# Up projection of a gated MLP by seven block products in place of eight, down projection in groups of two

## The chip, the cores and the metric

One core of one Trainium2 chip runs the whole program. The time is device microseconds of one execution of the program, from the first instruction to the last; the time before is the median of three runs. TensorE (PE in the profile; its weight loads are PEld) multiplies, VectorE (DVE) and ScalarE (ACT) work on tiles in SBUF and read PSUM, GpSimd (POOL) works on SBUF only, and SyncE (SP) issues most DMAs.

## The reference

A decoder layer on 2048 tokens of 1024 channels: a norm, an input projection, three token mixers, an output projection, then the gated MLP with a convolution of width 3 along the tokens, then a per-layer embedding and a last norm. The change touches the MLP:

```python
def conv_ffn(h, w_up, conv_w, w_down):
    gu = causal_dwconv(h @ w_up, conv_w)      # h: 2048 x 1024, w_up: 1024 x 5632
    g, u = jnp.split(gu, 2, axis=-1)
    return (jax.nn.silu(g) * u) @ w_down      # w_down: 2816 x 1024
...
x = x + conv_ffn(rmsnorm(x, norm_ffn_gain[i]), ffn_w_up[i], ffn_conv_w[i], ffn_w_down[i])
```

All data is float32.

## The kernel before

The sequence is worked in two halves of 1024 tokens, each in two chunks of 512 (`NC`). Channels lie on the 128 partitions, so x is eight tiles of 1024 tokens, and a projection's output comes channel tile by channel tile, tokens along the free axis. The loop `for hf in range(NH)` runs the mixers, the output projection, the MLP and the embedding of one half and then of the other.

Every operand of a large product is kept as two float32r parts, high and low: `split` (L151) copies the high part on ScalarE (L153) and subtracts it on VectorE for the low part (L154). `mm3` (L159) makes one float32 product of three matmuls, high by high, high by low, low by high (L160 to L162). One projection of a channel tile on one chunk is 8 x 3 matmuls of 512 columns into one PSUM bank.

Weights come in the order of their use (`wlist`). `w_issue` (L131) loads one raw tile through SP's queue into one of two raw buffers and splits it; `w_next` keeps two more in hand than the one taken. Split weights have their own pool of four double tiles (`wp`); activations share the 32 tiles of `bp`.

In the MLP, `up(j)` (L708) projects two channel tiles, j of g and j of u, into one double PSUM bank each (`mm`, two of them), on both chunks. `conv` (L299) reads PSUM: ScalarE applies the first tap (L303), VectorE the two others (L307), with two columns of the tokens before (L309) or for the tokens after (L311). Then SiLU on ScalarE (L737), the gate product (L738) and a split into `ahi` and `alo`. `down(js)` takes up to three such tiles (`JG = 3`): for each of eight output tiles and two chunks it accumulates 3 x 3 matmuls in one of four single banks (`sm`) and VectorE adds the bank to x (L753). The order of `up` and `down` is that of `ffn_order`; the last group is one tile, and its `down` also splits x for the next stage. The first `up` is spread so that the norm of the second chunk (`Norm.rstd`, `bcast`, `h_apply`, L317) has work of the first beside it.

The order written is a priority only. A planner sets each engine's order ahead of the run: an instruction whose inputs or whose buffer are not ready by its estimate is passed by a later one, so a weight split stands between two steps of a convolution and the MLP's first matmuls stand between the last of the output projection. Tiles of a pool are given to whoever comes when one is free.

Of the kernel before, what the change touches and what calls it, by code (L numbers as in the profile page):

```python
# [11 lines left out]
I32 = mybir.dt.int32  # L12
# [19 lines left out]
JG = 3  # L32

# columns of the per-channel vectors: one column per 128 channels
# [8 lines left out]
# columns of the shape-only constants  # L43
# [5 lines left out]
def trunk(ctx, tc, xT, pT, w_in, w_out, w_up, w_down, w_pp, w_pg, wr_bd, wi_bd, vecs, consts, masks, out):  # L49
# [3 lines left out]
    wp = ctx.enter_context(tc.tile_pool(name="wp", bufs=4))  # L53
    bp = ctx.enter_context(tc.tile_pool(name="bp", bufs=32))
# [38 lines left out]
    wlist = []  # L93

    def ffn_order():
        ev = []
        groups = [list(range(j0, min(j0 + JG, NJ))) for j0 in range(0, NJ, JG)]
        for gi, js in enumerate(groups):
            for i, j in enumerate(js):
                ev.append(("up", j, None))  # L100
                if gi > 0 and i == (0 if gi < len(groups) - 1 else len(js) - 1):
                    ev.append(("down", gi - 1, groups[gi - 1]))
        ev.append(("down", len(groups) - 1, groups[-1]))
        return ev

    def down_per(js):
        return {1: 8, 2: 4, 3: 2, 4: 2}[len(js)]
# [7 lines left out]

    IN_UNITS = [9, 6, 12, 15, 10, 7, 13, 16, 11, 8, 14, 0, 3, 1, 4, 2, 5, 20, 22, 18, 21, 23, 19, 17]
    for hf in range(NH):
        wlist += [kc(w_in[m]) for m in IN_UNITS]
        wlist += [kc(w_out[m]) for _ in range(NC) for m in range(KD)]
        for ev, i, js in ffn_order():  # L120
            if ev == "up":
                wlist += [kc(w_up[i]), kc(w_up[NJ + i])]
            else:
                per = down_per(js)
                for m0 in range(0, KD, per):
                    wlist.append(w_down[m0 : m0 + per, :, js[0] : js[-1] + 1, :].rearrange("m p j c -> p m (j c)"))
        wlist += [kc(w_pg[m]) for _ in ple_chunks(hf == NH - 1) for m in range(KD)]
    wq = []
    wpos = [0]

    def w_issue():  # L131
        if wpos[0] >= len(wlist):
            return
        src = wlist[wpos[0]]
        wpos[0] += 1
        w = wp.tile([P, 2, D], F32R, tag="w", name=nm("w"))
        raw = wp.tile([P, D], F32, tag="wr", name=nm("wr"), bufs=2)
        dst, n = raw, D
        if len(src.shape) == 3:
            n = src.shape[1] * src.shape[2]  # L140
            dst = dst[:, :n].rearrange("p (a b) -> p a b", b=src.shape[2])
        nc.sync.dma_start(dst, src)
        split(w[:, 0, :n], w[:, 1, :n], raw[:, :n])
        wq.append(w)

    def w_next(ahead=2):
        while len(wq) <= ahead and wpos[0] < len(wlist):
            w_issue()
        return wq.pop(0)

    def split(hi, lo, src, eng=None):  # L151
        """hi + lo <- src, in two float32r parts; src is float32."""
        i = ACT(hi, src, AF.Copy)  # L153
        last_split[:] = i, (eng or nc.vector).tensor_tensor(lo, src, hi.bitcast(F32), op=SUB)  # L154

    def wsl(w, k):
        return w[:, 0, k * P : (k + 1) * P], w[:, 1, k * P : (k + 1) * P]

    def mm3(ps, wk, rk, start, stop):  # L159
        MM(ps, wk[0], rk[0], start=start, stop=False)  # L160
        MM(ps, wk[0], rk[1], start=False, stop=False)  # L161
        MM(ps, wk[1], rk[0], start=False, stop=stop)  # L162
# [29 lines left out]
    class Norm:  # L192
        """1/rms over the channels of 512 tokens."""
# [36 lines left out]
    def head_norm(y, gain, scale=1.0):  # L230
        """y <- rmsnorm over each head's 64 channels of (scale * y), times gain; gain has scale in it."""
# [14 lines left out]
    def head_sum(parts, name):  # L246
        """1/64 of the sum over each head's 64 channels, on all of them."""
# [43 lines left out]
    rgw = cp.tile([P, 2, 2, 3, P], F32R, name="rgw")  # L291
    mk = cp.tile([P, NL - 1, C], I32, name="mk")
# [6 lines left out]
    def conv(dst, src, taps, bias, tail, first, last):  # L299
        """causal depthwise convolution along the free axis; taps[d]: the weight at delay d."""  # L300
# [12 lines left out]
    def h_apply(dst, xs, gain, pr, pool=()):  # L313
        """dst[k] <- xs[k] * gain * pr, in two parts; the k in pool have one step on GpSimd."""
# [56 lines left out]
    for hf in range(NH):  # L371
# [336 lines left out]
        def up(j, head=False):  # L708
# [10 lines left out]
            if head:  # L719
                for i in range(2):  # L720
                    ws[i], pss[i] = w_next(), ps2("pu2")
# [205 lines left out]
```

## Time and profile before

| | |
|---|---|
| median of three runs | 2584.52 us (2583.66 to 2589.34) |
| span of the profiled execution | 2585.0 us |
| first and last matmul of the MLP's up projection, both halves | 458 us, 2413 us |
| DMA over the span | 168.40 MB, mean 65 GB/s |
| instructions | 29876 |

The profile is of one execution. A row of a group gives the line, the engine, the operation, output and inputs, shapes and count; then the busy time, the mean of one instruction in ns, the idle time of the engine just before them, and what ended that. The ends of matmuls are modelled, and rows of matmuls overlap. The granted clock is given as a share of full speed. In a timeline, the first number is the start from the span's begin and the second the duration.

### The profile page before, as it was taken

To read this page: it belongs to the slowest core of one execution; us is meant where nothing else is said; L and a number is where in the kernel's file an instruction comes from. 1 tells how busy PE (TensorE), PEld (TensorE's weight loads), DVE (VectorE), ACT (ScalarE), POOL (GpSimd) and SP (SyncE) were. 2 spreads that over 40 slices of the span, in tenths; PEclk is the share of its full clock that TensorE was granted. 3 is DMA by queue.
4 is the path that set the end of the run, shared out by engine and by line. 5 is a ranking of instruction groups with operands and counts; after the bars stand their busy time and mean duration, and the time that the engine had idled before them with its cause. 6 is when DMAs were issued, how large, how long until landed. Compare 5 with 4: busy or idle time off the path is not lost.

```text
span 2585.0 us, 29876 instructions
## 1 busy us (share of the span) xinstructions
PE 2544.2 (98%) x12508; PEld 2106.3 (81%) x12508; DVE 1411.1 (55%) x1984; ACT 958.2 (37%) x1170; POOL 79.9 (3%) x94
## 2 busy tenths in 40 slices
PE   7999999999999999999999999999999999999998
PEld 5888788788888888888888887888888888888888
DVE  7666565653453443447666655665443453453666
ACT  5444873422122222224444458633222222121344
POOL 3000000200000000000110000000000000000000
PEclk9999999999999999999999999999999999999999
DMA  4111014321111111113420011331111111111224
GB/s 143 34 33 34 33 65 135 109 76 41 56 51 41 56 43 49 55 43 131 139 89 34 25 33 41 102 127 35 55 49 44 55 43 50 56 34 58 80 88 141
DMA packets 64663, 168.40 MB, mean 65 GB/s; under 512 B 6160, under 2 KB 27920, under 8 KB 64528
## 3 DMA queue, kind: packets, MB, share of 16 engines
q1 hardware_dynamic: 58960, 149.09, 17.7%
q0 software_dynamic: 4992, 16.78, 1.9%
q8 instruction: 98, 1.61, 0.3%
q10 hardware_dynamic: 576, 0.62, 0.1%
q14 instruction: 37, 0.30, 0.0%
HBM read 158.08 MB, written 8.39 MB: 64 GB/s over the span
## 4 chain that ended last, share of the span: by engine, by line
PE 90%; ACT 5%; DVE 3%; issue 1%; DMA 1%; POOL 0%; SPq 0%; DVEq 0%; POOLq 0%; ACTq 0%
PE pu L160 12%; PE pu L161 12%; PE pu L162 12%; PE pdn L160 6%; PE pdn L162 6%; PE pdn L161 6%; PE pz L160 5%; PE pz L161 5%; PE pz L162 5%; PE pgt L160 2%; PE pgt L161 2%; PE pgt L162 2%; PE po L160 2%; PE po L161 2%; PE po L162 2%; PE pl L535 2%
## 5 line engine op out<-in xcount | busy, mean ns | idle before, releaser
L160 PE MATMUL pu<-h,w 128*128 128x512 f32 x1408 | 548.5, 390 | 2.9 <-DVE ftail L311 2.6
L161 PE MATMUL pu<-h,w 128*128 128x512 f32 x1408 | 549.0, 390 | 0.6 <-POOL h L154 0.4
L162 PE MATMUL pu<-h,w 128*128 128x512 f32 x1408 | 548.2, 390 | 0.0
L307 DVE SCALAR_TENSOR_TENSOR gu<-pu,vt,gu 128x1023 f32<-128x1023 f32 (+1 forms) x176 | 225.1, 1279 | 517.3 <-ACT gu L303 517.3
L153 ACT ACTIVATE w<-wr 128x1024 fp32r<-128x1024 f32 (+1 forms) x266 | 267.9, 1009 | 381.9 <-PE pdn L162 299.0
L154 DVE TENSOR_TENSOR w<-wr,w 128x1024 fp32r<-128x1024 f32 (+1 forms) x266 | 309.8, 1165 | 48.4 <-ACT w L153 47.8
L160 PEld LDWEIGHTS pu<-h,w 128*128 128x128 f32 x1408 | 264.5, 188 | 58.3 <-ACT w L153 3.0
L161 PEld LDWEIGHTS pu<-h,w 128*128 128x128 f32 x1408 | 264.5, 188 | 57.4 <-POOL h L154 2.7
L160 PE MATMUL pz<-h,w 128*128 128x512 f32 x768 | 307.6, 401 | 2.5 <-ACT h L153 2.3
L162 PEld LDWEIGHTS pu<-h,w 128*128 128x128 f32 x1408 | 264.5, 188 | 54.7
L161 PE MATMUL pz<-h,w 128*128 128x512 f32 x768 | 303.4, 396 | 2.0 <-DVE h L154 1.7
L162 PE MATMUL pz<-h,w 128*128 128x512 f32 x768 | 301.4, 393 | 0.0
L160 PE MATMUL pdn<-ahi,w 128*128 128x512 f32 x704 | 274.3, 390 | 0.0
L162 PE MATMUL pdn<-ahi,w 128*128 128x512 f32 x704 | 274.3, 390 | 0.0
L161 PE MATMUL pdn<-alo,w 128*128 128x512 f32 x704 | 274.2, 390 | 0.0
L303 ACT ACTIVATE gu<-pu,vt 128x1024 f32<-128x1024 f32 x88 | 98.2, 1116 | 449.6 <-PE pu L162 449.6
L753 DVE TENSOR_TENSOR x<-x,pdn 128x512 f32<-128x512 f32 x256 | 173.0, 684 | 155.3 <-PE pdn L162 154.9
L160 PEld LDWEIGHTS pz<-h,w 128*128 128x128 f32 x768 | 145.4, 189 | 34.1 <-ACT h L153 3.6
L161 PEld LDWEIGHTS pz<-h,w 128*128 128x128 f32 x768 | 145.4, 189 | 34.0 <-DVE h L154 4.6
L162 PEld LDWEIGHTS pz<-h,w 128*128 128x128 f32 x768 | 145.3, 189 | 30.0
L162 PEld LDWEIGHTS pdn<-ahi,w 128*128 128x128 f32 x704 | 132.2, 188 | 27.5
L160 PEld LDWEIGHTS pdn<-ahi,w 128*128 128x128 f32 x704 | 132.2, 188 | 27.5
(218 smaller groups left out, 3088.8 us busy)
## 6 DMA issues: line engine op xcount, KB each, us to landing
wr<-in_w_up SPq DMA_DIRECT2D x88, 512.0 KB, 3.3
wr<-in_w_in SPq DMA_DIRECT2D x48, 512.0 KB, 3.3
wr<-in_w_down SPq DMA_DIRECT2D x56, 384.0 KB, 3.3
wr<-in_w_pg SPq DMA_DIRECT2D x40, 512.0 KB, 3.3
wr<-in_w_out SPq DMA_DIRECT2D x32, 512.0 KB, 3.4
xr<-in_xT POOLq DMA_DIRECT2D x32, 256.0 KB, 3.2
out_y<-o SPq DMA_DIRECT2D x24, 256.0 KB, 2.5
xl<-in_xT SPq DMA_DIRECT2D x8, 512.0 KB, 8.1
```

Of the source, the lines that this page charges most:

```text
L153: i = ACT(hi, src, AF.Copy)
L154: last_split[:] = i, (eng or nc.vector).tensor_tensor(lo, src, hi.bitcast(F32), op=SUB)
L160: MM(ps, wk[0], rk[0], start=start, stop=False)
L161: MM(ps, wk[0], rk[1], start=False, stop=False)
L162: MM(ps, wk[1], rk[0], start=False, stop=stop)
L303: ACT(dst, src, AF.Copy, scale=taps[0])
L307: STT(dst[:, d:TH], src[:, 0 : TH - d], taps[d], dst[:, d:TH], op0=MUL, op1=ADD)
L535: MM(pl[:, t * P : (t + 1) * P], K[:, tk : tk + P], qz[:, c * 4 + t].rearrange("p a b -> p (a b)"), start=True, stop=True)
L753: TT(x[m][:, cks(c)], x[m][:, cks(c)], ps, op=ADD)
```

## The change

For each channel tile pair but the first of each half, the eight block products of the up projection become seven. The blocks are: channel tiles g and u (weights wg, wu), halves of the 1024 input channels (a, b), and token chunks (0, 1). The inputs X1 and X2 are the halves of chunk 0, X3 the second half of chunk 1, and X4 to X7 sums and differences of the four, made once in `h2_first` and `h2_second`; the weights of products 3, 5, 6 and 7 are sums and differences of the four quarters of a raw pair, made for every tile by `job_s` on VectorE and then split. Products 1, 6, 7 and 4 accumulate into one bank A that is copied between them. The convolution reads the sums from SBUF. The first pair of each half uses `up_first`, eight products of which two have a difference of inputs.

Down groups are of two tiles, then two of one. Weights are named jobs in one list and taken with `w_get`, two jobs ahead. MLP weights take tiles of the pool `ff`, which is opened before the output projection with nine tiles; all other weights take tiles of `bp`, which has 40. Mask and gate weights of the mixers lie in the mixers' pool and are loaded in each half. The scratch for DMAs issued by GpSimd is smaller.

```diff
-    wp = ctx.enter_context(tc.tile_pool(name="wp", bufs=4))
-    bp = ctx.enter_context(tc.tile_pool(name="bp", bufs=32))
+    wp = ctx.enter_context(tc.tile_pool(name="wp", bufs=2))
+    bp = ctx.enter_context(tc.tile_pool(name="bp", bufs=40))
...
+    GROUPS = [[j, j + 1] for j in range(0, NJ - 2, 2)] + [[NJ - 2], [NJ - 1]]
...
+    def job_a(hf, j):
+        g = raws[hf, j, 0] = raw_w(kc(w_up[j]))
+        raws[hf, j, 1] = raw_w(kc(w_up[NJ + j]))
+        hi, lo = ftile("wh", F32R), ftile("wl", F32R)
+        split(hi, lo, g)
+        return hi, lo
...
+    def job_s(hf, j, which):
+        g, u = raws[hf, j, 0], raws[hf, j, 1]
+        hi, lo = ftile("wh", F32R), ftile("wl", F32R)
+        q = [slice(0, CH), slice(CH, D)]
+        if which == 0:
+            s = raws[hf, j, 2] = sp.tile([P, D], F32, tag="s", name=nm("s"), bufs=1)
+            TT(s[:, q[0]], u[:, q[0]], u[:, q[1]], op=ADD)
+            TT(s[:, q[1]], s[:, q[0]], g[:, q[0]], op=SUB)
+        else:
+            s = raws[hf, j, 2]
+            TT(s[:, q[0]], g[:, q[1]], s[:, q[1]], op=SUB)
+            TT(s[:, q[1]], g[:, q[0]], u[:, q[0]], op=SUB)
+        split(hi, lo, s)
+        return hi, lo
+
+    def job_a22(hf, j):
+        t = ftile("w22", F32R)
+        split(t[:, :CH], t[:, CH:], raws[hf, j, 1][:, CH:])
+        return t
...
+        for j in range(NJ):
...
+            wlist += [(("a", *a), lambda a=a: job_a(*a))]
+            wlist += [(("s", *a, i), lambda a=a, i=i: job_s(*a, i)) for i in range(2)]
...
+            if j % 2 == 0:
+                wlist.append(down[0])
+            wlist.append((("a22", *a), lambda a=a: job_a22(*a)))
+            if j % 2 == 0:
+                wlist.append(down[1])
...
+        def h2_second(pr):
...
+            for q in range(KQ):
+                hx(h1[q], q, 1, pr)
+                TT(h0[q], h1[q], h0[q], op=SUB)
+                X[5][q] = split_chunk(h0[q], "h")
+            yield
+            for q in range(KQ):
+                hx(h1[KQ + q], KQ + q, 1, pr)
+                X[3][q] = split_chunk(h1[KQ + q], "h")
+            yield
+            for q in range(KQ):
+                TT(h0[q], h1[KQ + q], h0[q], op=SUB)
+                nc.gpsimd.tensor_tensor(h1[q], h1[KQ + q], h1[q], op=SUB)
+                X[6][q] = split_chunk(h0[q], "h")
+            yield
+            for q in range(KQ):
+                nc.gpsimd.tensor_tensor(h0[KQ + q], h0[KQ + q], h0[q], op=SUB)
+                X[7][q] = split_chunk(h1[q], "h")
+            yield
+            for q in range(KQ):
+                X[4][q] = split_chunk(h0[KQ + q], "h")
...
+        def prod(ps, w, xs_, start, stop):
+            for q in range(KQ):
+                mm3(ps, (w[0][:, q * P : (q + 1) * P], w[1][:, q * P : (q + 1) * P]), hsl(xs_[q]),
+                    start and q == 0, stop and q == KQ - 1, skip_group_check=True)
...
+        def up(j, between):
+            A, BC = ps1(name="pa"), ps2("pbc")
+            B, Cc = BC[:, C0], BC[:, C1]
+            zg, zu = ftile("zg"), ftile("zu")
+
+            def p1():
+                prod(A, wa[0], X[1], True, False)
+                ACT(zg[:, C0], A, AF.Copy)
+
+            def p2():
+                prod(Cc, wa[1], X[2], True, True)
+                TT(zg[:, C0], zg[:, C0], Cc, op=ADD)
+
+            def p5():
+                prod(B, ws[0], X[5], True, False)
+                ACT(zu[:, C1], B, AF.Copy)
+
+            def p6():
+                prod(A, ws[1], X[6], False, False)
+                ACT(zg[:, C1], A, AF.Copy)
+
+            def p3():
+                prod(B, wt[0], X[3], False, True)
+                TT(zg[:, C1], zg[:, C1], B, op=ADD)
+
+            def p7():
+                prod(A, wt[1], X[7], False, False)
+                TT(zu[:, C1], zu[:, C1], A, op=ADD)
+
+            wa = halves(w_get("a", hf, j))
+            p1()
+            if between is None:
+                ws = halves(w_get("s", hf, j, 0))
+                p5()
+                p6()
+                p2()
+                wt = halves(w_get("s", hf, j, 1))
+                p7()
+                p3()
+                g = conv_g(j, zg)
+            else:
+                p2()
+                ws = halves(w_get("s", hf, j, 0))
+                p5()
+                p6()
+                wt = halves(w_get("s", hf, j, 1))
+                p3()
+                p7()
+                g = conv_g(j, zg)
+                between()
+            t = w_get("a22", hf, j)
+            prod(A, (t[:, :CH], t[:, CH:]), X[4], False, True)
+            ACT(zu[:, C0], A, AF.Copy)
+            conv_u(j, zu, g)
...
+        up_first()
+        for j in range(1, NJ):
+            up(j, (lambda gi=j // 2 - 1: down(gi)) if j % 2 == 0 else None)
```

`between` is the down projection of the two tiles before, in every even tile.

## Rows read from the trace of the kernel before

**Rows 1.** The page: busy shares; granted clock by slices (tenths); the ending chain's engines.

```profile
PE 2544.2 (98%) x12508; PEld 2106.3 (81%) x12508; DVE 1411.1 (55%) x1984; ACT 958.2 (37%) x1170; POOL 79.9 (3%) x94
...
PEclk9999999999999999999999999999999999999999
...
PE 90%; ACT 5%; DVE 3%; issue 1%; DMA 1%; POOL 0%; SPq 0%; DVEq 0%; POOLq 0%; ACTq 0%
```

**Rows 2.** TensorE's waits, longest first: total us, times, longest us.

```profile
PE pm L211 <- DVE sq L203: 14.9, 2, 12.4
PE pmh L249 <- ACT sqp L153: 5.0, 4, 2.3
```

**Rows 3.** MLP window: busy us (count) of PE, PEld, DVE, ACT, POOL; clock; DMA.

```profile
1800.00:2400.00 600.00, 600.00 (x2649) 497.26 (x2648) 271.60 (x343) 135.79 (x135) 0.00 (x0) 1.00 0.16 49
```

**Rows 4.** Groups by line, TensorE: count, busy us, mean ns, idle before.

```profile
L160 PE MATMUL pu<-h,w 128*128 128x512 f32 x1408 | 548.5, 390 | 2.9 <-DVE ftail L311 2.6 <-DVE gu L309 0.3
...
L160 PE MATMUL pdn<-ahi,w 128*128 128x512 f32 x704 | 274.3, 390 | 0.0
```

**Rows 5.** Groups by line and shape, VectorE.

```profile
L154 DVE TENSOR_TENSOR w<-wr,w 128x1024 fp32r<-128x1024 f32 x210 | 256.6, 1222 | 48.4 <-ACT w L153 47.8
L753 DVE TENSOR_TENSOR x<-x,pdn 128x512 f32<-128x512 f32 x256 | 173.0, 684 | 155.3 <-PE pdn L162 154.9
L307 DVE SCALAR_TENSOR_TENSOR gu<-pu,vt,gu 128x1023 f32<-128x1023 f32 x88 | 112.9, 1283 | 517.3 <-ACT gu L303 517.3
...
L154 DVE TENSOR_TENSOR h<-hx,h 128x512 fp32r<-128x512 f32 x45 | 37.0, 837 | 0.2
...
L528 DVE TENSOR_TENSOR Q<-Q,T 128x512 f32<-128x512 f32 x30 | 20.9, 698 | 4.8 <-ACT qz L526 4.8
L154 DVE TENSOR_TENSOR xs<-x,xs 128x512 fp32r<-128x512 f32 x32 | 20.3, 685 | 0.6 <-ACT xs L153 0.6
...
L309 DVE SCALAR_TENSOR_TENSOR gu<-ftail,vt,gu 128x2 f32<-128x2 f32 x44 | 9.3, 211 | 0.0
...
L311 DVE COPY ftail<-pu 128x2 f32<-128x2 f32 x44 | 6.6, 150 | 0.0
...
L307 DVE SCALAR_TENSOR_TENSOR ysc<-cc,vt,ysc 128x1023 f32<-128x1023 f32 x4 | 5.1, 1283 | 0.3 <-ACT ysc L303 0.2
```

**Rows 6.** VectorE in order of time, one tile of MLP: start, duration (us).

```profile
1093.26 1.28 DVE L307 SCALAR_TENSOR_TENSOR gu<-pu,vt,gu 128x1023 f32<-128x1023 f32 x1 [9.66 <-ACT gu L303]
1094.46 1.22 DVE L154 TENSOR_TENSOR w<-wr,w 128x1024 fp32r<-128x1024 f32 x1
```

**Rows 7.** Groups by line and shape, ScalarE.

```profile
L153 ACT ACTIVATE w<-wr 128x1024 fp32r<-128x1024 f32 x210 | 221.1, 1055 | 381.9 <-PE pdn L162 299.0 <-PE po L162 69.2 <-PE pz L162 6.0
...
L241 ACT ACTIVATE sqh<-pmh,epsc 128x512 f32<-128x512 f32 x32 | 20.5, 685 | 13.3 <-PE pmh L250 13.1
...
L303 ACT ACTIVATE ysc<-cc,vt 128x1024 f32<-128x1024 f32 x4 | 4.6, 1146 | 0.4 <-DVE cc L453 0.4
```

**Rows 8.** DMA issues of the MLP's weights: size, us from issue to landing.

```profile
wr<-in_w_up SPq DMA_DIRECT2D x88, 512.0 KB, 3.3
```

**Rows 9.** Groups by line and shape, the head's scaling on VectorE and GpSimd's part.

```profile
L154 POOL TENSOR_TENSOR h<-hx,h 128x512 fp32r<-128x512 f32 x19 | 29.8, 1569 | 108.5 <-ACT h L153 108.4
...
L317 DVE SCALAR_TENSOR_TENSOR hx<-x,vt,pr 128x512 f32<-128x512 f32 x32 | 22.7, 741 | 2.9 <-PE pr L227 2.9
```

**Rows 10.** Windows over the MLP's head, first and second half (columns as rows 3).

```profile
470.00:500.00 30.00, 27.04 (x122) 20.91 (x121) 21.61 (x32) 14.87 (x20) 8.75 (x9) 1.00 0.29 95
1740.00:1800.00 60.00, 59.45 (x267) 48.16 (x266) 35.44 (x50) 23.04 (x27) 6.26 (x4) 1.00 0.14 41
```

**Rows 11.** VectorE in order of time: one low part at the head.

```profile
477.41 1.12 DVE L154 TENSOR_TENSOR h<-hx,h 128x512 fp32r<-128x512 f32 x1
```

**Rows 12.** A window over the MLP's tail, first half (columns as rows 3).

```profile
1180.00:1200.00 20.00, 20.00 (x90) 16.49 (x89) 20.00 (x33) 13.02 (x21) 1.43 (x2) 1.00 0.27 92
```

More of the change, by code (lines that the diff above doesn't have):

```diff
@@ L90, in cks, with ftile @@
         return slice(c * CH, (c + 1) * CH)
[L93 to L107, printed above, removed]
+    pools = {}
+    def ftile(name, dt=F32):
+        return pools["ff"].tile([P, TH], dt, tag="ff", name=nm(name))
+    GROUPS = [[j, j + 1] for j in range(0, NJ - 2, 2)] + [[NJ - 2], [NJ - 1]]
     def ple_chunks(last):
@@ L114, in kc, with raw_w, whole @@
         return w.rearrange("p k c -> p (k c)")
+    def raw_w(src):
+        raw = wp.tile([P, D], F32, tag="wr", name=nm("wr"))
+        dst = raw if len(src.shape) == 2 else raw.rearrange("p (a b) -> p a b", b=src.shape[2])
+        nc.sync.dma_start(dst, src)
+        return raw
+    def whole(src, tile_of):
+        raw = raw_w(src)
+        hi, lo = tile_of("wh", F32R), tile_of("wl", F32R)
+        split(hi, lo, raw)
+        return hi, lo
+    raws = {}
+    def job_a(hf, j):
[4 more added lines that the diff above has]
+        return hi, lo
@@ L116, in trunk, with job_d @@
+    def job_a22(hf, j):
+        t = ftile("w22", F32R)
+        split(t[:, :CH], t[:, CH:], raws[hf, j, 1][:, CH:])
+        return t
+    def job_d(hf, js, m0, per):
+        return whole(w_down[m0 : m0 + per, :, js[0] : js[-1] + 1, :].rearrange("m p j c -> p m (j c)"), ftile)
     IN_UNITS = [9, 6, 12, 15, 10, 7, 13, 16, 11, 8, 14, 0, 3, 1, 4, 2, 5, 20, 22, 18, 21, 23, 19, 17]
+    wlist = []
     for hf in range(NH):
-        wlist += [kc(w_in[m]) for m in IN_UNITS]
-        wlist += [kc(w_out[m]) for _ in range(NC) for m in range(KD)]
@@ L120, in trunk @@
[L120 to L128, printed above, removed]
-    wpos = [0]
[L131 to L149, printed above, removed]
+        wlist += [(("in", hf, m), lambda m=m: whole(kc(w_in[m]), t4)) for m in IN_UNITS]
+        wlist += [(("out", hf, c, m), lambda m=m: whole(kc(w_out[m]), t4)) for c in range(NC) for m in range(KD)]
+        for j in range(NJ):
+            a = (hf, j)
+            if j == 0:
+                wlist += [(("a", *a), lambda a=a: job_a(*a)), (("u", *a), lambda a=a: job_u(*a))]
+                continue
+            wlist += [(("a", *a), lambda a=a: job_a(*a))]
+            wlist += [(("s", *a, i), lambda a=a, i=i: job_s(*a, i)) for i in range(2)]
+            down = [(("d", hf, j // 2 - 1, i), lambda a=hf, js=GROUPS[j // 2 - 1], i=i: job_d(a, js, 4 * i, 4)) for i in range(2)]
+            if j % 2 == 0:
[3 more added lines that the diff above has]
+                wlist.append(down[1])
@@ new lines, in trunk, with w_upto @@
+        wlist += [(("d", hf, gi, 0), lambda a=hf, js=GROUPS[gi]: job_d(a, js, 0, 8)) for gi in range(len(GROUPS) - 2, len(GROUPS))]
+        wlist += [(("pg", hf, t, m), lambda m=m: whole(kc(w_pg[m]), t4)) for t in range(len(ple_chunks(hf == NH - 1))) for m in range(KD)]
+    wat = {key: i for i, (key, _) in enumerate(wlist)}
+    wmade = {}
+    wpos = [0]
+    def w_upto(n):
+        while wpos[0] < min(n, len(wlist)):
+            key, job = wlist[wpos[0]]
+            wpos[0] += 1
+            wmade[key] = job()
@@ L151, in split, with w_get @@
+    def w_get(*key, ahead=2):
+        w_upto(wat[key] + 1 + ahead)
+        return wmade.pop(key)
     def split(hi, lo, src, eng=None):
@@ L328, in stats_stream @@
         return n
-    def stats_stream(hf, c):
-        n = Norm()
-        for k in range(KD):
-            s = t2("xs")
-            nc.gpsimd.dma_start(s, xT[k, :, hf * TH + c * CH : hf * TH + (c + 1) * CH])
-            n.add(s)
-        n.rstd()
-        return n
     nc.vector.memset(epsc, EPS)
@@ L386, in trunk, with mixer_consts @@
         z = {}
+        rgw = mx.tile([P, 2, 2, 3, P], F32R, name=nm("rgw"))
+        mk = mx.tile([P, NL - 1, C], I32, name=nm("mk"))
+        def mixer_consts():
+            nc.scalar.dma_start(mk, masks)
+            for i, src in enumerate((wr_bd, wi_bd)):
+                t = t4("rgw")[:, : 3 * P].rearrange("p (a b) -> p a b", b=P)
+                nc.scalar.dma_start(t, src)
+                split(rgw[:, i, 0], rgw[:, i, 1], t)
         def hg_f(j, ps):
@@ L657, in trunk @@
         mx.release()
+        pools["ff"] = ff = tc.alloc_tile_pool(name=f"ff{hf}", bufs=9)
         x = [None] * KD
-        h = [[None] * KD for _ in range(NC)]
         def out_evac(c, m, ps, n):
@@ L680, in trunk @@
                 if c == 0 and m0 == 0:
-                    ws = [w_next(), w_next()]
+                    ws = [w_get("out", hf, c, m) for m in range(2)]
                     for i in range(2):
```

157 lines of the change are left out of this document (88 added, 69 removed).

## The prediction

> **What bounds the kernel now.** I read the page from the top: busy shares, then the chain that ended last, then the waits of TensorE, then one steady stretch of the MLP by windows. TensorE is busy 98% of the span, the chain is TensorE for 90%, and its clock is granted in full in all 40 slices [rows 1]. Its waits for other engines are few: 14.9 us at the very first norm, then nothing above 5.0 us in total for a pair of lines [rows 2]. So the time is TensorE's, and what counts is the time from one matmul to the next. That is not the 390 ns mean of a matmul's row: in 600 us of MLP 2649 matmuls ran, one per 0.2265 us [rows 3]; their rows overlap. In the same stretch VectorE is busy 271.6 of 600 us (45%) and ScalarE 136 us (23%).
>
> **What is removed.** The up projection has 1408 x 3 matmuls of 512 columns, 96 for each of 22 channel tiles in each half, the down projection 704 x 3 [rows 4]. Seven products of 4 x 3 matmuls take the place of eight in 21 tiles (the first tile keeps all eight), so 12 x 21 x 2 = 504 matmuls go: 504 x 0.2265 = 114.2 us, all on the path. The down projection keeps its 2112 matmuls; only their groups change (6 in place of 9 to a PSUM bank). By the mean of a row it would be 197 us; the rows overlap, so the spacing decides.
>
> **What is added beside it.** Per two channel tiles (one step of the new loop: an odd tile, an even tile, one down group) VectorE does, at the durations of [rows 5]: 10 low parts of 1024 columns (three of weights per tile, two of down weights, two of activations) 10 x 1.22 = 12.2; two half-width low parts 2 x 0.69 = 1.4; eight sums and differences of weights, 8 x 0.70 = 5.6; six additions of PSUM products, 6 x 0.68 = 4.1; eight convolution steps 8 x 1.28 = 10.2 (the same from SBUF as from PSUM); the tails 0.6 in the first half, 8 x 0.21 = 1.7 in the second; two gate products at the price of a low part, 2.4; 16 additions of the down projection 16 x 0.68 = 10.9. Sum 47.4 to 48.5 us. Instructions that follow each other start about 0.08 us earlier than the durations say (one of 1.28 us, the next 1.20 us after it [rows 6]); for 52 of them that is 4 us, so 43.5 to 44.5 us of VectorE. TensorE needs 2 x 84 + 96 = 264 matmuls, 59.8 us. VectorE goes from 45% to about 74%, ScalarE (eight high parts of weights at 1.06, two of half width and eight PSUM copies of 512 at 0.69, four convolution starts at 1.15, four more of 1.06; [rows 7]) to 24 us, 40%. Neither passes TensorE, so all of this is hidden as long as no single chain is late. If that cover were gone, VectorE's 24 us a tile would be the pace, still under TensorE's 29.9.
>
> **The chains that TensorE now waits for.** Before, products went into two double banks and TensorE ran far ahead. Now bank A takes four products one after another and is copied in between, and the weights of products 3, 5, 6 and 7 are computed by VectorE from two raw buffers.
> - Bank A. Between a product and the next one into A lies at least one other product, 12 x 0.2265 = 2.7 us; the copy takes 0.69 on ScalarE behind at most one instruction of 1.15 [rows 7], or 0.68 on VectorE behind one of 1.28 [rows 5]. Slack 0.7 to 0.9 us: hidden, mostly.
> - Weight sums, the late one. In an even tile, count from the end of the odd tile's last-but-one product. TensorE has product 4 of the old tile and products 1, 2, 5, 6 of the new: 5 x 2.72 = 13.6 us until it needs the second pair of weight sums. VectorE has in that time, by spacing: add 0.6, first pair of sums 1.2, convolution of g 2.4, low part 1.1, convolution of u 2.4, gate product 1.1, low part 1.1, second pair 1.2, low part 1.1, tails 0.3 to 0.8, and waits for ScalarE twice (1.06 each, partly covered): 12.5 to 14.5 us. It is about just in time. The odd tile has the down projection ahead of it and 1.5 us to spare.
> - Raw weights: 3.3 us from issue to landing [rows 8], two loads per tile, and the buffers come free when the second sums and the half-width split are done, some 6 us before the next use: hidden.
> - Three banks are left for the down projection in an even tile (A holds the fourth): 3 x 6 x 0.2265 = 4.1 us for an addition of 0.68 behind one or two of 1.28: hidden.
> For these chains together the trace has no row. The ends are 0 and 3 us for each of the 20 steps (the second pair with nothing ahead of it in time: sums 1.2, high part 1.06, low part 1.1); I take 0.9 a step, near the lower end since the counted slack is about nil rather than negative: 18 us.
>
> **The head of the MLP.** The second chunk's norm feeds 20 split tiles in place of eight: 8 scalings of 0.74, 8 differences and 20 low parts on VectorE, 8 differences on GpSimd [rows 9]. TensorE has as before the first chunk's 48 matmuls ahead of it, then products of X5 and X3 (10.9 us) and products 1, 2, 5 and 6 of the next tile (10.9 us) before it needs that tile's second weight sums. VectorE by then has, by spacing, X5 and X3 12.6, X6 5, additions and g's convolution 3.6, X7 and X4 4.9, u's part 4.7, sums and low parts 4.7: 35.5 us, if the planner leaves the order as written. Against 22 to 24 us that is up to 12 us a half; before, TensorE lost 3.0 us there in the first half and 0.5 in the second (30 less 27.0, 60 less 59.45 [rows 10]). I take 7 in each: +10.5 us (0 to 22).
> A rule speaks against this place. Row first: low parts on VectorE take 0.84 us on the mean of these lines, 1.12 for one that ran beside GpSimd, and 0.69 elsewhere [rows 5, 11]; 8 GpSimd differences so cost some 8 x 0.44 = 3.5 us a half, part of the 7. The Trainium skill (SBUF — State Buffer, "Who interferes with whom") says that a VectorE instruction with two SBUF inputs and a GpSimd instruction that reads SBUF exclude each other for the whole instruction. Taken to the letter it makes the price a whole GpSimd instruction each time; that is a rival below.
>
> **The tail of the MLP.** The last two tiles go down one by one: 32 additions and 16 low parts of x behind u's 4.7 us, by spacing 4.7 + 48 x 0.6 = 33.5 us of VectorE over 96 matmuls (21.7 us). Before, the group of three covered the first half of that, and VectorE was full for 20 us while TensorE kept working on the next stage [rows 12]. That filler is there still, but the first split x comes after 4.7 + 9.6 + 1.2 = 15.5 us against 10.9 + 2.7 of work: 2 us, and I add 1 for the small weights that now wait for the pool of the MLP: 3 a half, +6 us (0 to 24).
> The 64 additions more per half are in the VectorE sum. Weights of the other stages now come from the shared pool (40 in place of 32 + 4 double): same bytes, two jobs ahead as before, so no cost; a split that came late would show its 1.06 and 1.22 us [rows 5, 7]. The mask and gate weights are loaded once more, four channel tiles of the input projection (4 x 48 x 0.2265 = 43 us) ahead of use. The smaller scratch I cost at nothing too: GpSimd is busy 80 us of the span [rows 1] and its loads are far from TensorE's path.
>
> **Sum.** Against the profiled span of 2585.0 us (the median of the runs is 2584.52, the same): 2585.0 - 114.2 + 18 + 10.5 + 6 = **2505 us**, 3% less.
>
> **Rivals.**
> - Everything hides: the planner fills each gap with another ready product. 2585 - 114 = 2471, to 2488 with heads and tails. For it: TensorE shows no gap in 600 us of MLP now [rows 3]; against: it was never in a loop with VectorE. Chance 0.2.
> - VectorE's latency sets the pace: every step loses 2.2 to 4.5 us, 44 to 90 us in all, 2531 to 2577. For it: 74% busy with instructions of 1.2 us and a chain with no slack. Chance 0.17.
> - VectorE stands through every GpSimd difference of the head, 1.57 us each [rows 9] in place of the 0.44 counted: 8 x 1.13 x 2 = 18 us more, 2523. Chance 0.06; the 1.12 us row speaks against it [rows 11]. This is the rule of "Who interferes with whom", taken to the letter.
> - Slower: the second weight sums are exposed in every tile, not every second, with the half-width split and the next raw load behind them, because two raw buffers keep the planner from running ahead: 1.2 + 1.06 + 1.1 of sums plus the odd tile's landing of 3.3, 3.4 to 6.7 us. It decides from 114.2 / 42 = 2.7 us a tile; at 3.4 it gives 2585 - 114 + 143 + 16 = 2630. Against: the first pair of sums and the next tile's raw weights have 8 us and more. Chance 0.06.
> - No change (2580 to 2590): 0.03, a point in between.
>
> **How the numbers follow.** My own case (2489 to 2530) has 0.48. Faster by over 0.2%, which is what can be told from no change: 0.48 + 0.2 + 0.17 + 0.06 = 0.91; same 0.03; slower 0.06. The range leaves out the end of the first rival (0.04), the slow third of the second (0.06), no change and slower (0.09): 2474 to 2562.
>
> **What would show it.** pu rows at 3 x 1240 matmuls with 0.2265 us spacing; VectorE at 70 to 78% between 520 and 1100 us; TensorE waiting for VectorE by some 0 to 3 us a step, at the second weight sums in even tiles first; gaps of 5 to 12 us in all just after the MLP's start. Wrong, if TensorE waits above all at bank A's copies or at raw loads, if its clock falls, or if the mixer stages get longer.

## The result and the profile after

The changed kernel takes 2679.1 us (2676.2 to 2680.6, four runs) against 2584.6 us: 1.036 times the time before, 95% interval 1.0345 to 1.0374. It is slower where 2505 us was forecast. The profiled execution has a span of 2676.7 us, 91.7 more than before.

The page, beside [rows 1]: 504 matmuls fewer, and TensorE at 93% in place of 98; the ending chain is TensorE for 54% in place of 90; in two slices the granted clock is under nine tenths.

```profile
PE 2491.7 (93%) x12004; PEld 2023.8 (76%) x12004; DVE 1803.4 (67%) x2530; ACT 1130.0 (42%) x1442; POOL 91.4 (3%) x102
...
PEclk9999999899999999999999999998999999999999
...
PE 54%; DVE 14%; ACT 9%; issue 2%; DMA 0%; ACTq 0%; DVEq 0%; SPq 0%
```

TensorE's waits, beside [rows 2] (total us, times, longest). The first line is new and larger than all others together: matmuls into bank A wait for ScalarE's copy of product 1 out of that bank (L849).

```profile
PE pa L203 <- ACT zg L849: 102.3, 31, 11.7
PE pm L254 <- DVE sq L246: 15.4, 4, 12.1
PE pbc L203 <- ACT zu L857: 12.7, 21, 0.8
PE pdn L203 <- DVE x L907: 10.5, 9, 2.3
```

Windows of the MLP, first and second half, columns as [rows 3]: where 2649 matmuls ran in 600 us, 2345 run in the second half. VectorE is at 70% and 67%, some 45 us of each step where 43.5 to 44.5 were counted, and not full.

```profile
520.00:1140.00 620.00, 579.03 (x2492) 467.05 (x2491) 432.52 (x549) 219.49 (x261) 4.85 (x9) 0.99 0.17 52
1850.00:2450.00 600.00, 556.10 (x2345) 446.73 (x2344) 401.24 (x531) 193.14 (x227) 0.00 (x0) 0.95 0.15 46
```

Where the time went, from the starts of the first product and of the last down matmul in each half (us; "shared" and "best" are experiments 12 and 11):

| stretch | before | after | shared | best |
|---|---|---|---|---|
| to the first product | 458.1 | 465.5 | 459.9 | 458.0 |
| MLP, first half | 737.4 | 761.0 | 718.0 | 708.5 |
| to the second half's first product | 534.7 | 537.8 | 537.6 | 539.2 |
| MLP, second half | 732.8 | 785.5 | 707.0 | 704.4 |
| rest | 122.1 | 126.9 | 127.1 | 125.3 |
| span | 2585.0 | 2676.7 | 2549.6 | 2535.4 |

Each half saves 57.1 us by its matmuls and yet is 23.6 and 52.7 longer: it loses 80.7 and 109.8 us.

**One wait, followed back.** TensorE, one matmul a row: the first of product 6, one step apart. A step is 64.8 us in the first half and 68.2 in the second, where its matmuls need 59.8. Behind the second half's gap of 4.62 us rows take 0.80 us and matmuls start 0.43 apart until 1981.42, the lower level of TensorE's clock (granted 0.50 from 1977.0 to 1981.4).

```profile
681.86 0.50 PE L203 MATMUL pa<-h,wh 128*128 128x512 f32 x1 [2.62 <-ACT zg L849]
...
746.65 0.50 PE L203 MATMUL pa<-h,wh 128*128 128x512 f32 x1 [2.62 <-ACT zg L849]
...
1908.93 0.80 PE L203 MATMUL pa<-h,wh 128*128 128x512 f32 x1 [4.62 <-ACT zg L849]
...
1977.13 0.80 PE L203 MATMUL pa<-h,wh 128*128 128x512 f32 x1 [4.62 <-ACT zg L849]
```

ScalarE ahead of two of these, in order of time. Product 1 had ended by 1969.8; yet the copy (L849) starts at 1976.50, for `ahi` and the high part of the second weight sums stand ahead of it, and ScalarE idles 4.46 us until VectorE has the gate product. In the first half only the sums' high part stands ahead (idle 2.53).

```profile
741.47 1.06 ACT L803 ACTIVATE gu<-gu 128x1024 f32<-128x1024 f32 x1 [1.05 <-DVE gu L348]
745.06 1.06 ACT L196 ACTIVATE wh<-s 128x1024 fp32r<-128x1024 f32 x1 [2.53 <-DVE s L148]
746.02 0.58 ACT L849 ACTIVATE zg<-pa 128x512 f32<-128x512 f32 x1
...
1969.07 1.06 ACT L803 ACTIVATE gu<-gu 128x1024 f32<-128x1024 f32 x1 [0.17 <-DVE gu L350]
1974.59 1.06 ACT L196 ACTIVATE ahi<-gu 128x1024 fp32r<-128x1024 f32 x1 [4.46 <-DVE gu L808]
1975.55 1.04 ACT L196 ACTIVATE wh<-s 128x1024 fp32r<-128x1024 f32 x1
1976.50 0.58 ACT L849 ACTIVATE zg<-pa 128x512 f32<-128x512 f32 x1
```

VectorE in the same stretch (its first and last steps of the block): it works without a pause from the convolution to the second sums (L148).

```profile
737.82 1.28 DVE L348 SCALAR_TENSOR_TENSOR gu<-zg,vt,gu 128x1023 f32<-128x1023 f32 x1 [1.02 <-ACT gu L344]
...
744.34 0.68 DVE L148 TENSOR_TENSOR s<-wr,wr 128x512 f32<-128x512 f32 x1
...
1973.34 1.22 DVE L808 TENSOR_TENSOR gu<-gu,gu 128x1024 f32<-128x1024 f32 x1
1974.47 0.68 DVE L148 TENSOR_TENSOR s<-wr,wr 128x512 f32<-128x512 f32 x1
```

Why can't TensorE do product 5 meanwhile? Its bank and product 2's are the two halves of one double tile, and the trace shows the two behind each other's readers: in an odd tile product 2 (in the bank Cc) waits for the copy of bank B. In the even tile product 5 comes at 748.15, in the middle of product 6, right behind VectorE's addition that reads product 2.

```profile
727.42 0.50 PE L203 MATMUL pbc<-h,wh 128*128 128x512 f32 x1 [0.46 <-ACT zu L857]
...
748.15 0.40 PE L203 MATMUL pbc<-h,wh 128*128 128x512 f32 x1
```

```profile
747.29 0.68 DVE L853 TENSOR_TENSOR zg<-zg,pbc 128x512 f32<-128x512 f32 x1
```

The start has a wait of its own: the first matmul of the input projection starts at 26.76 us (20.4 before), since SP's queue has one raw weight more ahead of the second chunk's x.

### The profile page after: what moved, and what is told of

It is laid out like the page before. It is cut to its first block, busy times and chain, and to the rows that moved or that the text cites. A ratio compares the mean times of both kernels' runs of the same rounds, so it can differ in the third digit from the quotient of the medians.

```text
span 2676.7 us, 29689 instructions
## 1 busy us (share of the span) xinstructions
PE 2491.7 (93%) x12004; PEld 2023.8 (76%) x12004; DVE 1803.4 (67%) x2530; ACT 1130.0 (42%) x1442; POOL 91.4 (3%) x102
## 4 chain that ended last, share of the span: by engine, by line
PE 54%; DVE 14%; ACT 9%; issue 2%; DMA 0%; ACTq 0%; DVEq 0%; SPq 0%
PE pdn L203 6%; PE pdn L204 5%; PE pdn L205 5%; DVE gu L348 5%; PE pa L203 3%; PE pbc L203 3%; PE pa L204 3%; PE pa L205 3%; PE pbc L204 3%; PE pbc L205 3%; PE pz L203 2%; PE pz L205 2%; PE pz L204 2%; DVE wl L197 2%; PE pgt L203 2%; PE pgt L205 2%
## 5 line engine op out<-in xcount | busy, mean ns | idle before, releaser
L197 DVE TENSOR_TENSOR wl<-wr,wh 128x1024 fp32r<-128x1024 f32 x210 | 256.2, 1224 | 97.9 <-ACT wh L196 97.7
L203 PE MATMUL pz<-h,wh 128*128 128x512 f32 x768 | 306.9, 400 | 9.6 <-ACT h L196 9.6
L203 PE MATMUL pa<-h,wh 128*128 128x512 f32 x536 | 218.9, 408 | 103.8 <-ACT zg L849 102.3
L204 PE MATMUL pz<-h,wh 128*128 128x512 f32 x768 | 303.1, 395 | 1.7 <-DVE h L197 1.4
L205 PE MATMUL pz<-h,wl 128*128 128x512 f32 x768 | 301.5, 393 | 0.0
L203 PE MATMUL pdn<-ahi,wh 128*128 128x512 f32 x704 | 279.6, 397 | 10.5 <-DVE x L907 10.5
L205 PE MATMUL pdn<-ahi,wl 128*128 128x512 f32 x704 | 276.2, 392 | 0.0
L204 PE MATMUL pdn<-alo,wh 128*128 128x512 f32 x704 | 276.2, 392 | 0.0
L196 ACT ACTIVATE wh<-wr 128x1024 fp32r<-128x1024 f32 x210 | 218.3, 1052 | 79.3 <-DMA wr<-in_w_down 34.1
L203 PE MATMUL pbc<-h,wh 128*128 128x512 f32 x536 | 219.6, 410 | 15.0 <-ACT zu L857 12.7
L204 PE MATMUL pbc<-h,wh 128*128 128x512 f32 x536 | 215.4, 402 | 4.5 <-DVE h L197 4.5
L204 PE MATMUL pa<-h,wh 128*128 128x512 f32 x536 | 212.9, 397 | 0.0
L203 PEld LDWEIGHTS pz<-h,wh 128*128 128x128 f32 x768 | 145.4, 189 | 41.1 <-ACT h L196 10.8
L204 PEld LDWEIGHTS pz<-h,wh 128*128 128x128 f32 x768 | 145.6, 190 | 33.3 <-DVE h L197 4.3
```

The lines of the kernel that those rows point to most:

```text
L203: MM(ps, wk[0], rk[0], start=start, stop=False, **kw)
L204: MM(ps, wk[0], rk[1], start=False, stop=False, **kw)
L205: MM(ps, wk[1], rk[0], start=False, stop=stop, **kw)
```

## The experiments

Ratios are to the kernel before. "On" names the kernel that was edited.

**1. Ten shared tiles** (on the changed kernel; to make room, a state that the mixers carry from half to half is left out).

```diff
-    scar = cp.tile([P, 3, C], F32, name="scar")
+        scar = mx.tile([P, 3, C], F32, name=nm("scar"))
...
-        pools["ff"] = ff = tc.alloc_tile_pool(name=f"ff{hf}", bufs=9)
+        pools["ff"] = ff = tc.alloc_tile_pool(name=f"ff{hf}", bufs=10)
```

> The changed kernel with ten tiles instead of nine in the MLP's pool; to make room, the state of the HGRN heads isn't carried from the first half to the second (that part of the computation is left out). Theory S (slots): the first copy of bank A into zg waits for a tile that the tile before holds until its u is convolved, so TensorE idles 2.6 us a step in the first half and 4.6 us in the second (and runs at a lower clock behind that). By S one tile more takes most of it away: step from 64.8 and 68.3 us to 60 to 62, time 2679 to about 2570 to 2600. Theory B (the two banks of one double tile wait for each other's readers) and theory V (VectorE is late with the convolution itself) expect under 25 us from it.

2672.7 us, 1.0335 [1.0319, 1.0351]. The gaps at the heads fall from 11.7 to 7.7 us and from 8.9 to 5.8, those of 2.6 and 4.6 in the steps stay (2.69 and 4.68). Slots are not the cause in the steps.

**2. Own banks** (on the changed kernel).

```diff
-            A, BC = ps1(name="pa"), ps2("pbc")
-            B, Cc = BC[:, C0], BC[:, C1]
+            A, B, Cc = ps1(name="pa"), ps2("pb")[:, C0], ps2("pc")[:, C0]
```

> The changed kernel with products 2 and 3/5 in two separate double tiles (one bank of each used), so that product 5 need not wait for the addition that reads product 2. By B product 5 (2.72 us) can stand in front of product 6 and fills the gap: 2.6 us less a step in the first half, 2.7 and some clock in the second: 2679 to about 2590 to 2615. By S alone the copy comes no sooner, but the gap is also covered; what is left would be some 2 us a step in the second half. By V nothing is gained beyond 20 us, since other products wait for the sums then.

2579.2 us, 0.997 [0.9959, 0.9981]: 100 us faster than the changed kernel. TensorE, the second half: product 5 (pb) now runs in the gap, and what is left of it is 4.62 - 12 x 0.2265 = 1.90 us.

```profile
2042.64 0.39 PE L205 MATMUL pb<-h,wl 128*128 128x512 f32 x1
2044.94 0.50 PE L203 MATMUL pa<-h,wh 128*128 128x512 f32 x1 [1.90 <-ACT zg L848]
```

The first half's 2.62 us are less than product 5 and vanish. ScalarE's order is as in the changed kernel, the copy as late. So the banks decide whether TensorE has something to do meanwhile, and not whether the copy is late.

**3. Weight jobs one ahead** (on the changed kernel), so that the second sums are written behind the copy.

```diff
-        w_upto(wat[key] + 1 + ahead)
+        w_upto(wat[key] + 1 + (1 if key[0] in ("a", "s", "a22", "d") and key[0] != "u" and key[2] > 0 else 2))
```

> The changed kernel with MLP weights prepared one job ahead instead of two. By S this leaves two tiles of the pool free for longer, the wait for the copy of bank A shrinks and the time falls to 2600 to 2650. By V (too much work of VectorE in too short a stretch) the sums now come too late and the time rises above 2700.

2657.8 us, 1.0278 [1.0261, 1.0295]. The waits show what was exchanged: the copy's fell from 102.3 to 13.1 us, and TensorE waits for low parts of weights instead, 37.1 us in 37 places.

```profile
PE pa L205 <- DVE wl L197: 20.8, 20, 1.8
PE pbc L205 <- DVE wl L197: 16.3, 17, 1.6
...
PE pa L203 <- ACT zg L849: 13.1, 2, 7.0
```

The 13.1 us are the two heads. In the first half's steps little comes in exchange: from 560 to 1080 us all waits fall from 32.3 to 10.0 us, and TensorE does 2199 matmuls where the changed kernel does 2116. The instructions and the banks are the changed kernel's; only the order differs. On ScalarE the copy now stands ahead of `ahi` and of the sums' high part and waits for neither.

```profile
560.00:1080.00 520.00, 509.32 (x2199) 405.82 (x2198) 369.84 (x475) 183.15 (x215) 0.00 (x0) 1.00 0.15 49
```

```profile
852.28 0.58 ACT L849 ACTIVATE zg<-pa 128x512 f32<-128x512 f32 x1
855.38 1.06 ACT L196 ACTIVATE ahi<-gu 128x1024 fp32r<-128x1024 f32 x1 [2.52 <-DVE gu L808]
...
857.06 1.05 ACT L196 ACTIVATE wh<-s 128x1024 fp32r<-128x1024 f32 x1
```

The waits for low parts are in the second half's steps, which gain almost nothing.

**4. Groups of two alone** (on the kernel before).

```diff
-JG = 3
+JG = 2
```

> The kernel before with down groups of two in place of three and nothing else. All theories: 64 more additions of 0.68 us in each half are hidden under TensorE, 2580 to 2590. If it were above 2600, the grouping would be a cause of its own.

2590.8 us, 1.0018 [1.0008, 1.0027]: some 4 us of the loss come from the grouping, if it costs the same in both kernels.

**5. x first** (on experiment 2).

```diff
-    w_upto(2)
     x_load(x0[1], 0, 1, nc.sync)
+    w_upto(2)
```

> Products 2 and 5 in banks of their own (as in the run that gave 2579 us), and at the very start the second chunk of x is loaded ahead of the second raw weight. Theory S: the first input-projection matmul starts at 26.8 us there in place of 20.4 before, because one raw weight more stands ahead of the second chunk's x in SP's queue; the 6.4 us go and nothing else changes: 2573. Rival: that start is paid by another wait (the second chunk's norm is late anyway, or the first weights then come late), first matmul at 25 to 27 us and 2577 to 2581.

2571.4 us, 0.9939 [0.9924, 0.9953]: 7.8 us faster, the first matmul at 20.1 us.

**6. The two columns of the half before left out** (on experiment 2).

```diff
-            if not first:
+            if not first and ends:
                 STT(dst[:, 0:d], tail[:, n - 1 - d : n - 1], taps[d], dst[:, 0:d], op0=MUL, op1=ADD)
```

> Own banks for products 2 and 5, and the MLP's convolutions of the second half leave out the two columns that come from the half before (88 x 2 small VectorE instructions of 0.21 us; that part of the result is left out). It asks why a step of two tiles costs 60.9 us in the first half and about 63.3 in the second. Theory V (VectorE's block of convolutions, sums and gate product sets when ScalarE reaches the copy of bank A): 4 x 0.13 us of block a tile less, so the gap of 2.1 us a step before product 6 shrinks to 1.0 to 1.5 and the half clock behind it (1.9 us in two steps of three) goes with it: 2579 - 10 x (0.8 + 1.3) = 2558 (2550 to 2565). Rival: the second half's gap has another cause (the order of the engines differs, no next half's statistics to load), the ends are hidden: 2577 to 2580.

2550.0 us, 0.9858 [0.9844, 0.9873], 29 us faster for some 88 x 0.13 = 11 us of VectorE. The number is theory V's and its reason is not: ScalarE's order in the second half changed. Beside the rows above, `ahi` now stands behind the copy, as in the first half, and product 5 covers the rest.

```profile
2022.05 1.06 ACT L803 ACTIVATE gu<-gu 128x1024 f32<-128x1024 f32 x1 [1.05 <-DVE gu L348]
2025.64 1.06 ACT L196 ACTIVATE wh<-s 128x1024 fp32r<-128x1024 f32 x1 [2.52 <-DVE s L148]
2026.61 0.58 ACT L848 ACTIVATE zg<-pa 128x512 f32<-128x512 f32 x1
2027.08 1.05 ACT L196 ACTIVATE ahi<-gu 128x1024 fp32r<-128x1024 f32 x1
```

**7. Weight sums on GpSimd** (on experiment 2).

```diff
-            TT(s[:, q[0]], u[:, q[0]], u[:, q[1]], op=ADD)
+            nc.gpsimd.tensor_tensor(s[:, q[0]], u[:, q[0]], u[:, q[1]], op=ADD)
```

(and so the other three of `job_s`)

> Own banks for products 2 and 5, and the weight sums and differences (8 of 0.68 us a step) run on GpSimd, which is idle in the MLP. Theory V: VectorE is 5.5 us a step shorter, most of it in the block ahead of the copy of bank A; gaps before product 6 below 0.8 us in both halves, steps of 60 to 61 us: 2579 - 10 x 2.7 - 10 x 0.5 = 2547. Theory O (it is ScalarE's fixed order, high part of the activations ahead of the copy): the gate product comes 0.7 us earlier only, gaps of 1.3 in the second half: 2565. Rival L: VectorE's low parts and convolutions beside GpSimd take 1.5 times as long, as the one at the head did, so VectorE gains nothing and the sums come later (3 us for a pair): 2585 to 2620.

2598.0 us, 1.0039 [1.0025, 1.0054]: 19 us slower with less work on VectorE. VectorE's own prices stay (low parts 1.22, convolutions 1.28 us; only its steps of one and two columns go from 0.21 to 0.48). So rival L, whose range this meets, is wrong on VectorE and right on the late sums; GpSimd's rows of the second half (1850 to 2430 us) show their price:

```profile
L148 POOL TENSOR_TENSOR s<-wr,wr 128x512 f32<-128x512 f32 x18 | 32.2, 1787 | 1.4
L147 POOL TENSOR_TENSOR s<-wr,s 128x512 f32<-128x512 f32 x18 | 32.1, 1782 | 86.6 <-DVE wl L197 86.6
L142 POOL TENSOR_TENSOR s<-wr 128x512 f32<-128x512 f32 x18 | 23.3, 1293 | 371.4 <-DMA wr<-in_w_up 352.1 <-DVE x L906 19.3
```

A second pair takes 3.6 us in place of 1.4, its high part stands ahead of copies on ScalarE, and TensorE waits 21.1 us at product 1's and 26.5 at product 5's.

**8. One ahead with own banks** (on experiment 2, the edit of 3).

```diff
-        w_upto(wat[key] + 1 + ahead)
+        w_upto(wat[key] + 1 + (1 if ... else 2))
```

> Own banks for products 2 and 5, and the MLP's weight jobs are issued one ahead in place of two, so that the second weight sums are written behind the copy of bank A. With shared banks this took the wait at that copy from 102 to 13 us, brought 37 us of waits for low parts of weights, and won 21 us. Theory O: the waits at the copy (25 us) go, and with the other banks as fillers the late low parts cost under 10: 2560. Theory V: the low parts come late by as much as before, since VectorE is the one that is late: 35 us of them for 25: 2585 to 2595.

2602.7 us, 1.0059 [1.0044, 1.0074]. The low parts come as late as in 3 (20.6 us at one line): two orders, two different waits.

**9. Two columns in front** (on experiment 5): the same result as before, without the small steps.

```diff
+        z = pools["ff"].tile([P, TH + 2], F32, tag="ff", name=nm(name))
+            nc.gpsimd.memset(z[:, 0:2], 0.0)
...
+            nc.gpsimd.tensor_copy(z[:, 0:2], ftail[:, m, :])
...
+                STT(t, zt[:, 2 - d : 2 - d + TH], vec("fcw", m * 3 + 2 - d), t, op0=MUL, op1=ADD)
```

> Own banks and x loaded first (2571 us), and the tiles of the MLP's products are two columns wider: GpSimd, idle there, puts the two columns of the half before (zeros in the first half) in front, so each convolution step on VectorE is one instruction over 1024 columns and its small ones of 0.21 us go, with the same result. Theory V (VectorE's block ahead of the copy of bank A): as where the columns were left out, which gave 29 us: 2571 - 29 = 2542 (2537 to 2549). Rival: GpSimd's two-column copies become a wait of their own, or hold up VectorE beside them as larger ones did (0.47 for 0.21): 2555 to 2572.

2545.7 us, 0.9843 [0.9829, 0.9858]; from 560 to 1100 and from 1810 to 2350 us TensorE has no wait.

The edit has a price too. Two windows of 480 us in the second half, first of experiment 6, which still waits for 2.1 us in it, then of this one, which doesn't: it does fewer matmuls.

```profile
1850.00:2330.00 480.00, 477.86 (x2080) 387.83 (x2079) 348.53 (x409) 171.34 (x201) 0.00 (x0) 1.00 0.16 52
```

```profile
1850.00:2330.00 480.00, 480.00 (x2070) 387.99 (x2069) 348.76 (x408) 172.61 (x202) 18.85 (x32) 1.00 0.16 51
```

In experiments 9 to 12 the MLP's matmuls start 0.232 us apart where nothing waits, in the other runs 0.227, with the clock granted in full. The input projection, whose weights lie in the other pool, stays at 0.227 in both. Matmuls beside GpSimd's small steps and away from them are equally slow. So the wider tiles are the suspect, which no run tests alone; over some 5980 matmuls of both MLPs it is about 28 us.

**10. Two plain tiles at the head** (on experiment 9).

```diff
-            if j == 0:
+            if j <= 1:
...
+        up_plain(1)
+        for j in range(2, NJ):
```

> As the run with the two columns in front, and the second channel tile of each half is projected plainly too (eight products), so that it needs only the first four activation tiles. Theory H (at the head VectorE has 35 us of splits and sums against some 23 us of TensorE's work): 21.8 us of matmuls more to stand beside it, for 24 matmuls more, 5.4 us; the head loses some 20 and 14 us of the two halves there, of which 25 come back: 20 us faster than the run with the two columns, 2522. Rival N: the loss is the norm of the second chunk and the first splits, ahead of any tile: 0 to 5 us slower. Rival S: nine shared tiles don't hold the weights of two plain tiles, which come late: 5 to 15 us slower.

2548.1 us, 0.9847 [0.9833, 0.9862], no difference from 9: about as much is won at the head as its 24 matmuls cost. Theory H's 20 us are not there.

**11. Differences on VectorE** (on experiment 9).

```diff
-                nc.gpsimd.tensor_tensor(h1[q], h1[KQ + q], h1[q], op=SUB)
+                TT(h1[q], h1[KQ + q], h1[q], op=SUB)
```

(and the same for X4's difference)

> As the run with the two columns in front, and the eight differences of activations at the head run on VectorE in place of GpSimd. Theory L (the two exclude each other: low parts and scalings of 0.7 us take 1.2 to 1.4 there): some 16 of them gain 0.5 us, 8 differences of 0.6 come on top: 3 us a half faster, 2536. Theory H (VectorE's sheer work at the head): 4.8 us a half more of it, 2545 to 2552.

2536.2 us, 0.9805 [0.9788, 0.9821], the fastest of all. VectorE's groups between 470 and 520 us, first of experiment 9, then of this one: 20 low parts cost 18.9 us beside GpSimd and 13.1 without it.

```profile
L205 DVE TENSOR_TENSOR h<-h,h 128x512 fp32r<-128x512 f32 x20 | 18.9, 988 | 0.9 <-ACT h L204 0.8
```

```profile
L205 DVE TENSOR_TENSOR h<-h,h 128x512 fp32r<-128x512 f32 x20 | 13.1, 686 | 0.5 <-ACT h L204 0.3
```

**12. The shared double tile again** (on experiment 11): the edit of 2 taken back.

> The run that gave 2536 us (x first, two columns in front, differences on VectorE) with one thing put back: products 2 and 5 in the two banks of one double tile, as in the changed kernel. It asks whether the shared tile or VectorE's late block is the root. Theory V (root is the late copy of bank A; the tile only took the filler away): with the shorter block the copy comes in time and no filler is needed; 0.5 us a step for product 2 behind the copy of product 5: 2536 + 20 x 0.5 = 2546 to 2552. Theory B (the tile costs by itself: product 5 stands behind the addition of product 2, each of them behind the other's reader): 3 us and more a step whatever VectorE does: 2600 to 2630. Between 2552 and 2600: both, TensorE's order with the shared tile has nothing ahead of product 6 and the copy is still late by some of it.

2549.5 us, 0.986 [0.9844, 0.9877]. With the banks of the changed kernel, only 13 us are lost to experiment 11. Here is the first half again, ScalarE and then VectorE:

```profile
707.35 1.16 ACT L807 ACTIVATE gu<-zg,vt 128x1024 f32<-128x1024 f32 x1 [7.21 <-DVE zg L878]
...
712.12 0.60 ACT L862 ACTIVATE zg<-pa 128x512 f32<-128x512 f32 x1 [0.98 <-PE pa L213]
712.61 1.05 ACT L816 ACTIVATE gu<-gu 128x1024 f32<-128x1024 f32 x1
715.91 1.06 ACT L204 ACTIVATE wh<-s 128x1024 fp32r<-128x1024 f32 x1 [2.25 <-DVE s L156]
```

```profile
708.61 1.28 DVE L809 SCALAR_TENSOR_TENSOR gu<-zg,vt,gu 128x1024 f32<-128x1024 f32 x1 [1.29 <-ACT gu L807]
...
715.14 0.68 DVE L156 TENSOR_TENSOR s<-wr,wr 128x512 f32<-128x512 f32 x1
```

VectorE is no faster: from the convolution's first step to the second sums it takes 715.14 - 708.61 = 6.53 us, in the changed kernel 744.34 - 737.82 = 6.52. ScalarE still idles 2.25 us for the sums. But the copy stands ahead of them and waits for TensorE alone, and the windows have one wait of 0.7 us in 540 us of the first half and one of 0.3 in the second:

```profile
560.00:1100.00 540.00, 539.19 (x2323) 433.33 (x2322) 390.29 (x467) 202.59 (x240) 20.02 (x75) 1.00 0.16 54
1810.00:2350.00 540.00, 539.72 (x2318) 433.62 (x2317) 389.50 (x453) 198.51 (x233) 19.40 (x36) 1.00 0.16 52
```

So theory V's number came in by another way than it said: no shorter block, another order. This run changes other things beside the order (columns, the head); against these as the cause stands the first half, which has no two-column steps to lose (only copies of 0.17 us) and whose VectorE block is the same to 0.01 us. Experiment 3's first half is the case where nothing but the order of the jobs differs, and there too the waits at the copy are gone.

## Why the prediction was wrong

**Right.** 504 matmuls went, and where nothing waits the others start 0.227 us apart; VectorE's share (70% in the first half, 67% of the second's longer steps, forecast 70 to 78) and its prices (1.22, 0.69, 1.28 us) held. The sentence on what would prove it wrong named both things that happened: waits at bank A's copies, and a falling clock.

**The step that failed: "Bank A."** It priced the copy at nothing: 2.7 us of another product between, a copy of 0.69 "behind at most one instruction of 1.15". The cover held at its least: product 2 stood between products 1 and 6 (741.15 to 743.64), and product 5, which the written order also puts there, did not, being behind product 2's reader. What failed is the copy. Ahead of it on ScalarE stood one or two high parts that were themselves waiting for VectorE, 2.5 or 4.5 us, so the queue's wait counted and not its work: from the modelled end of product 1 to the end of the copy it took 5.3 us in the first half (741.31 to 746.60) and 7.3 in the second (1969.79 to 1977.08), where at most 1.15 + 0.69 = 1.84 was forecast. The prediction's sum for all chains, 18 us, met 10 x (64.8 - 59.8) + 10 x (68.2 - 59.8) = 134 us. The second half's part holds the clock: beyond the waits, matmuls there lost 23 us to spacing above 0.2265.

The Trainium skill (PSUM — Partial Sum Buffer, "Engine vs sequencer instructions") says that ScalarE's queue is strictly first in, first out. The trace agrees: at 1970.1 a copy whose product had ended stood 6.4 us behind two instructions that waited.

**"Weight sums, the late one."** The chain was rightly counted as having no slack, and the late data were VectorE's. But it was looked for at TensorE (weights that come late) and not at the engine between, which takes the sums' high part. In experiments 3 and 8, with another order, that wait at TensorE did come, 37 us in 3, nearly all of it in the second half.

**Head and tail.** Of the 190.5 us that both MLPs lose, 56 are not in the steps, where 16.5 were forecast. The largest pieces are one gap of 11.7 us behind the copy in the first head and one of 8.9 in the second: the term "Bank A" again. With banks of their own (experiment 2) the same two are 2.4 and 0.5 us, and other waits of 2 to 3 us appear. In the head's VectorE sum the 0.44 us a difference for GpSimd's company was too small: experiment 11 took 9.5 us away, 4.7 a half, by removing it.

The rival for that company, from "Who interferes with whom" in the Trainium skill's SBUF — State Buffer, has the mechanism right and the price too high. At both heads of the changed kernel 15 VectorE instructions with two SBUF inputs start while a GpSimd difference runs, and all 15 end 0.54 to 0.55 us behind it, whether they then took 1.12 us or 1.78. Two that read PSUM (L835) keep their 0.67 us. One of the 15, VectorE and then GpSimd, with ends at 1798.70 and 1798.15:

```profile
1796.95 1.75 DVE L740 TENSOR_TENSOR h<-h,h 128x512 f32<-128x512 f32 x1
```

```profile
1796.50 1.65 POOL L746 TENSOR_TENSOR h<-h,h 128x512 f32<-128x512 f32 x1 [0.63 <-DVE h L740]
```

The 1.12 us row that the prediction held against the rival is the same case: it ended at 478.53, GpSimd's at 477.98. The price is lower because VectorE gets there 0.4 to 1.2 us after GpSimd has begun: in the first half the 20 low parts cost 5.8 us more beside GpSimd's eight differences, 0.73 for each of these, between the 0.44 counted and the rival's 1.57. The section adds that the order of issue decides which of the two is held up; in experiment 7 GpSimd was the slower one (1.79 us for the second pair, 1.29 for the first), which fits but doesn't show the order.

**The start** stood in no term of the sum; a queue that the edit passed, SP's, held x back by 6.4 us (experiment 5: 7.8).

**The rivals.** "Everything hides" came true for the waits in the steps in experiments 9 and 12, once the order was another, but not for the time (2546 and 2549 us, its 2471 to 2488 forecast). The slower rival had the right sign, and its 143 us for the tiles is near the 134 measured by luck: the exposure was at ScalarE's copy, not at raw loads.

**Still open.** The best kernel still misses the matmuls' 114.2 us by 65. Both MLPs gain 57.4 and so still lose 57. Against 0.2265 us a matmul 17 us are lost at the heads, 18 at the tails and 24 in the steps between (2241 and 2245 matmuls in two windows of 520 us that have waits of 2.1 us in all), less 2 that the kernel before loses too. What the steps lose is nearly all the wider spacing that came with experiment 9. The stretches outside are 8 us longer than before. Only two changes of the head were tried on any of this.

## What to carry to other kernels

For each copy that frees a bank, list what stands ahead of it on its engine and for which engine each of these waits; an instruction's price there is its wait, not its duration. Before counting a neighbouring product as cover, look whether its bank is free by itself, or part of a tile whose other half is being read. Where a planner sets the order, look at the order of the engine in between (here ScalarE) first: an edit elsewhere that flips it may be worth more than the work it saves.

## What the runs showed of the hardware

- After a gap of 4.62 us TensorE's matmuls started 0.43 us apart, the lower of its two levels, for 4.3 us (granted 0.50). After those of 2.62 in the first half they did so once, from 616.2, and eight times not (as at 746.65, granted 1.00). After gaps of 1.9 in experiment 2 they did in some steps (from 2046.5 to 2049.5) and not in others (2108.86).
- A VectorE instruction of 512 columns with two SBUF inputs that starts while GpSimd runs a difference ends 0.54 to 0.55 us after GpSimd's, every time at the heads of the changed kernel; with one input in PSUM it took its usual 0.67 us.
- With weights in tiles two columns wider, matmuls of 512 columns start 0.232 us apart in place of 0.227, at a granted clock of 1.00 (experiments 9 to 12). Whether the width does it was not run alone.
- VectorE's instructions of 1.2 us kept their duration beside GpSimd's sums, while its steps of one and two columns went from 0.21 to 0.48 us; at the head it was VectorE's low parts of 512 columns that took longer.
